# Sample states of a gated linear attention layer, contracted in two rounds of four per head

## Chip, core and metric

The kernel runs on one core of one Trainium2 chip. The metric is the device time of one execution in microseconds. The core's engines are named as the profile names them: PE multiplies matrices (PEld is its weight load, PEq its sequencer), DVE and ACT do elementwise work, POOL here mainly issues transfers, SP issues the other transfers.

## The reference

One inference step of a trunk with two layers, for a prompt of 256 tokens and for 8 samples of one token each, all with the same weights. Layer 0 mixes by pooling, layer 1 by gated linear attention; each is followed by an MLP with squared ReLU, and each of the four parts by a layer norm. What the change touches is the attention of the 8 samples. There are 4 heads with keys of 256 and values of 512, and each sample brings a state S of 256 x 512 for each head:

```
proj = x @ w_in;  q, k, v, og, gk_low = split(proj)
log_a = log_sigmoid(gk_low @ w_gate_up + gate_bias) / 16
# one token of a sample, per head
S_new = exp(log_a)[:, None] * S + outer(k, v)       # an output: new_gla_sample
o     = (q / 16) @ S_new
# then, for prompt and samples
o = rms_norm(o) * norm_w * silu(og);  y = o @ w_out
```

The prompt's attention is computed in chunks and gives its own state; the change leaves that as it is.

## The kernel before

**Layout.** Activations lie transposed, features on the 128 partitions and 264 columns (256 prompt tokens and 8 samples). The weights are a stream of 1 MB units, each 128 output features by 2048 inputs: 128 units for the first MLP, 64 for attention (48 of w_in, 16 of w_out), 128 for the second MLP. A unit is loaded by SP into `raw` (two buffers), and each half is split into a rounded part `whi` (ACT, L132) and a rest `wlo` (DVE, L133), six buffers each. The activations are split in the same way, and `mm3` (L145 to L147) makes three products for each of a unit's 16 blocks: 48 products a unit, one behind the other on PE.

**Order of the work.** PE runs in the order in which the program writes its instructions. For the other engines and for SP's and POOL's queues a scheduler fixes the order ahead of the run, from program order and its own estimates of when things are ready. Within `project`, after each 12 products, `slot()` advances every generator in the list `background` to its next `yield`. All the attention work that is not a product of weights is written as such generators: `normalise` and `gate_up`, then `chain` for the prompt (one head after the other), `samples` for the samples (one head after the other, each after its values are `turned`) and `rms`. A `yield` is therefore a wait of 12 products on PE, and what a generator issues on PE stands between two groups of 12. A head's k, q and v are eight units, 32 slots.

**The samples of a head.** `turn` transposes the values and their rests to `vs`, 16 rows by 512. For each of the eight samples: the state is loaded as one tile of 2 x 512 columns (the 256 keys are two halves of 128 partitions), ACT multiplies it by the decay (L596), PE spreads one sample's value over all partitions by a product with a column of `pick` (L615, into the one buffer of the PSUM bank "mc"), DVE adds k times that value to each half (L618), POOL stores the new state (L619), and three slots later `contract` (L610) multiplies it with q: two products of 32 weight columns (q in `qpad`, one of them not zero) and 512 moving columns, which go to a group of 32 PSUM partitions in the bank "mb", the group being the sample's number modulo four. Then the state of the sample after next is loaded. There are three such tiles. The products of this part are float32 and appear as two records each; those of `mm3` and L615 are float32r and appear as one.

**The gate's low rank product** (`gate_low`, L391) comes once, ahead of this: 32 float32 products of 32 weight columns, written so that four successive ones go to the four groups of PSUM partitions.

Of the kernel before, what the change touches and what calls it, by code (L numbers as in the profile page):

```python
# [6 lines left out]
F32 = mybir.dt.float32  # L7
F32R = mybir.dt.float32r
# [5 lines left out]
P = 128  # L14
D = 2048
KT = D // P
NP = 256
# [34 lines left out]
def _body(ctx, tc, nc, a, o, stop):  # L52
# [26 lines left out]
    def prm(name, i):  # L79
        return par[:, OFF[name] + i:OFF[name] + i + 1]  # L80

    # two sets of 16 tiles in two float32r parts; a pair of tiles is one slot of a set
    def hslot(s, i, shape, dt, name):
        return hp.tile(shape, dt, name=name, tag=f"{s}{i}")

    class Parts:
# [4 lines left out]
            for i in pairs:  # L91
                self.fresh(i)

        def fresh(self, i):
            th = hslot(self.s, i, [P, 2, NX], F32R, "hh")
            tl = hslot(self.s, 8 + i, [P, 2, NX], F32R, "hl")
            self.pairs[i] = th, tl
            for e in range(2):
                self.hi[2 * i + e], self.lo[2 * i + e] = th[:, e], tl[:, e]
# [1 line left out]
        def pair(self, m):  # L101
            return self.pairs[m // 2]

# [1 line left out]
    units = []  # L105

    def mlp_units(l):
# [75 lines left out]
        V.scalar_tensor_tensor(t, v, EPS, t, ALU.add, ALU.mult)  # L183
        V.scalar_tensor_tensor(out, t, 1.5, y0, ALU.add, ALU.mult)

    # ---- layer norm over the partitions of all tiles of Z + the last products.
    # d = z - c with c the mean of the first half; y = (d r - m) g + b. The next products take
    # g d, with g and b as two more columns, and are put right by r and m where they are read.
    class Norm:
        def __init__(self, name, x, ahead=1):  # L190
            self.g, self.b = name.replace("_", "_g"), name.replace("_", "_b")
# [165 lines left out]
    def gla(gctx, norm, xp, x, hg):  # L357
        gp = gctx.enter_context(tc.tile_pool(name="gp", bufs=1))
        masks = gp.tile([P, 576], U8, name="masks")
        wup = gp.tile([P, HEADS * DK], F32, name="wup", tag="s0", bufs=3)  # L360
        nwh = gp.tile([P, 4], F32, name="nwh")
        mf = gp.tile([P, 576], F32, name="mf", tag="s0", bufs=3)
        nc.gpsimd.dma_start(mf, a["masks"])
        V.tensor_copy(masks, mf)
        nc.sync.dma_start(wup, a["wup"])
        V.tensor_scalar(nwh, par[:, OFF["norm_w"]:OFF["norm_w"] + 4], 0.5, None, ALU.mult)
        rr = [gp.tile([P, N], F32, name=f"rr{i}") for i in range(2)]
        sa = gp.tile([P, 8, NS], F32, name="sa")
# [8 lines left out]
        wg = gp.tile([P, KT * 32], F32, name="wg", tag="st", bufs=2)  # L377
        low = gp.tile([P, N], F32, name="low", tag="st", bufs=2)
        nc.sync.dma_start(wg, a["wgk"])
        pick = gp.tile([2 * NS, NS], F32R, name="pick")  # L380
        G.tensor_tensor(pick, ident[:2 * NS, :NS], ident[:2 * NS, NS:2 * NS], op=ALU.add)

        # gate: log_a * 16 = min(gk, 0) - ln(1 + exp(-|gk|)); the low rank in four groups of columns,
        # summed by the product with the gate's weights
        def gate_low():
            ps = bank("mc")[:, :NX]
            for j in range(4):
# [8 lines left out]
        def gate_up():  # L396
            tc.keep_in_program_order(S.preload_act_table_set("natural_log_exp_and_others"))
            for t in range(8):
                yield
                while norm.done <= t:  # L400
                    yield
                ps = bank("ma")[:, :N]
                PE.matmul(ps, lhsT=wup[:, t * P:(t + 1) * P], rhs=low, start=True, stop=True)
                b = prm("gate_bias", t)
                e = wtile()
                S.activation(e, ps, AF.Abs, bias=b)
                S.activation(e, e, AF.Exp, scale=-1.0)
                S.activation(e, e, AF.Ln, bias=1.0)
                V.tensor_scalar(LA[:, t], ps, b, 0.0, ALU.add, ALU.min)
                V.tensor_tensor(LA[:, t], LA[:, t], e, op=ALU.subtract)  # L410
            S.activation(sa, LA[:, :, NP:], AF.Exp, scale=SCALE)
# [7 lines left out]
        class Head:  # L419
# [64 lines left out]
            def value(self, t, ps, raw):  # L484
                v = wtile()
                evacuate(v, ps, raw)

                vp = work.tile([P, 2 * NS], F32R, name="vp", bufs=4)
                V.tensor_copy(vp[:, :NS], v[:, NP:])
                V.tensor_tensor(vp[:, NS:], v[:, NP:], vp[:, :NS].bitcast(F32), op=ALU.subtract)  # L490

                def turn():
                    if t == 0:
                        self.vtok = [hslot(hg, 8 + 2 * self.h + b, [P, DV], F32, "vtok") for b in range(2)]
                        self.vs = gp.tile([2 * NS, DV], F32R, name="vs", bufs=2)
                    tp = bank("ma")
                    for b in range(2):
                        PE.transpose(tp[:, b * P:b * P + P], v[:, b * P:b * P + P], ident)  # L498
                    PE.transpose(tp[:2 * NS, NP:NP + P], vp.bitcast(F32), ident)
                    c = slice(t * P, t * P + P)  # L500
                    for b in range(2):
                        V.tensor_copy(self.vtok[b][:, c], tp[:, b * P:b * P + P])
                    S.copy(self.vs[:, c], tp[:2 * NS, NP:NP + P])
                    self.turned = t + 1

                if not raw:
                    later(2, turn)
                else:
                    self.turns = getattr(self, "turns", []) + [turn]
                    if t == 3:  # L510
                        for e, fn in enumerate(self.turns):
                            later(2 + e, fn)
# [53 lines left out]
            def rms(self):  # L566
# [18 lines left out]
                self.normed = True  # L585
                yield

            def samples(self):
                h = self.h
                s0s = {}  # L590

                def load(b):
                    s0s[b] = gp.tile([P, 2, DV], F32, name="s0", bufs=3)
                    nc.sync.dma_start(s0s[b], a["st"][h, b])
                    for hf in range(2):
                        S.mul(s0s[b][:, hf], s0s[b][:, hf], sa[:, 2 * h + hf, b:b + 1])  # L596

                load(0)
                load(1)
                while self.turned < 4:  # L600
                    yield
                for r in range(2):
                    V.tensor_copy(qpad[:, :, 4 * r:4 * r + 4, r], self.q[:, :, NP + 4 * r:NP + 4 * r + 4])
                yield
                op = bank("mb")

                def contract(b):
                    c, r = b % 4, b // 4
                    for hf in range(2):
                        PE.matmul(op[32 * c:32 * c + 32], lhsT=qpad[:, hf, b], rhs=s0s[b][:, hf],  # L610
                                  start=r == 0 and hf == 0, stop=r == 1 and hf == 1, tile_position=(0, 32 * c))

                for b in range(NS):
                    vb = bank("mc")
                    PE.matmul(vb, lhsT=pick[:, b:b + 1].broadcast_to([2 * NS, P]), rhs=self.vs, start=True, stop=True)  # L615
                    s0 = s0s[b]
                    for hf in range(2):
                        V.scalar_tensor_tensor(s0[:, hf], vb, self.k[:, hf, NP + b:NP + b + 1], s0[:, hf], ALU.mult, ALU.add)  # L618
                    nc.gpsimd.dma_start(o["ngs"][h, b], s0)  # L619
                    yield  # L620
                    yield
                    yield
                    contract(b)
                    if b + 2 < NS:
                        load(b + 2)
                    for _ in range(PACE_B[b % 2]):
                        yield
                os_ = gp.tile([P, DV], F32, name="os", tag="st", bufs=2)
                S.copy(os_, op)
                yield  # L630
                yield
                tp = bank("ma")
                for t in range(4):
                    PE.transpose(tp[:, t * P:t * P + P], os_[:, t * P:t * P + P], ident)
                tv = tp.rearrange("p (t c r) -> p t r c", t=4, c=4)
                V.tensor_copy(self.oT[:, :, NP:].rearrange("p t (r c) -> p t r c", r=2), tv[:, :, :2])
                self.sampled = True
# [64 lines left out]
        for h in range(HEADS):  # L702
            for t in range(4):
# [1 line left out]
                while not heads[h].normed:  # L705
                    slot()
                if t == 0:
                    gated.fresh(2 * h)
                    gated.fresh(2 * h + 1)
                heads[h].gate(t, ps, gated)  # L710
        assert not background and not pending
        return gated

# [1 line left out]
    xs = Parts("a")  # L715
    with tc.tile_pool(name="poolp", bufs=2) as pp:
        band, xt = {}, {}
# [75 lines left out]
    ln = mlp(0, ln, xs, Parts("b"), lambda: Parts("a"))  # L793
    if stop == "mlp0":
        return dump(ln)
# [1 line left out]
    with ExitStack() as gctx:  # L797
        xr = Parts("b")
        gated = gla(gctx, ln, ln.x, xr, "a")
    for m in range(KT):  # L800
        S.mul(Z[m], xr.hi[m][:, :N].bitcast(F32), ALPHA)
        V.scalar_tensor_tensor(Z[m], xr.lo[m][:, :N].bitcast(F32), ALPHA, Z[m], ALU.mult, ALU.add)
    xs = Parts("b")
    tc.keep_in_program_order(S.preload_act_table(AF.Abs_reciprocal_sqrt))
    ln = Norm("mix_1", xs)
    for m in range(KT):
        ln.add(project(gated))
    if stop == "gla":
        return dump(ln)
    ln = mlp(1, ln, xs, Parts("a"), None)  # L810
# [95 lines left out]
```

## Time and profile before

| | |
|---|---|
| time, median of 3 runs | 2137.87 us (2137.3 to 2138.28) |
| span of the profiled execution | 2137.0 us |
| PE busy | 2112.2 us, 99% of the span |
| DVE busy | 1255.9 us, 59% |
| ACT busy | 1081.8 us, 51% |
| HBM | 362.65 MB read, 22.14 MB written |

The span is that of one profiled execution, from its first to its last instruction; its time as the runs count it is not shown apart from that, and the median of the runs stands 0.87 us above the span. Busy times are unions of the records of an engine. A PE record is longer than the pace at which PE takes the next one, since matmuls are pipelined; the pace is read from start to start. One record of L145 lasts 288 ns in the mean, for example.

### The profile page before, as it was taken

What the parts mean: (1) busy time and instruction counts of PE and PEld (TensorE: products, weight loads), DVE (VectorE), ACT (ScalarE), POOL (GpSimd) and SP (SyncE); (2) the same over time, 40 slices, a digit from 0 to 9 for tenths busy, and PEclk for the clock granted to TensorE, in tenths of its full rate; (3) what the DMA queues carried; (4) which work ended last, traced back from release to release, by engine and by line L of the source; (5) the groups of instructions that cost most, each with busy time, mean ns of one, the idle gap of its engine ahead of it and who ended that gap; (6) DMA issues with size and microseconds to landing.
All of it is one profiled execution on the core that took longest, in us unless ns stands there. A gap on an engine that the chain in (4) does not pass through costs nothing.

```text
span 2137.0 us, 38691 instructions
## 1 busy us (share of the span) xinstructions
PE 2112.2 (99%) x16436; PEld 2029.0 (95%) x16436; DVE 1255.9 (59%) x1964; ACT 1081.8 (51%) x1650; POOL 37.1 (2%) x96
## 2 busy tenths in 40 slices
PE   8999999999999999999999999999999999999996
PEld 7999999999999999987878799999999999999996
DVE  3966444444544578856566667876444444444565
ACT  3657354345335456645545555557355345435543
POOL 0000000000000000000000010000000000000000
PEclk9999999999999999999999999999999999999998
DMA  6554555555554454555555544455555555555442
GB/s 233 179 182 180 180 181 181 180 179 178 177 178 178 178 178 158 188 208 211 202 198 199 206 163 175 169 178 177 180 181 180 181 180 180 179 178 178 178 178 81
DMA packets 62189, 386.18 MB, mean 181 GB/s; under 512 B 6752, under 2 KB 11104, under 8 KB 20528
## 3 DMA queue, kind: packets, MB, share of 16 engines
q1 hardware_dynamic: 56480, 363.27, 48.1%
q0 software_dynamic: 5392, 20.28, 2.4%
q8 instruction: 128, 2.10, 0.4%
q14 instruction: 45, 0.37, 0.1%
q10 hardware_dynamic: 144, 0.16, 0.0%
HBM read 362.65 MB, written 22.14 MB: 180 GB/s over the span
## 4 chain that ended last, share of the span: by engine, by line
PE 97%; DVE 1%; DMA 1%; ACT 1%; SPq 0%; issue 0%; ACTq 0%; DVEq 0%
PE ps L145 30%; PE ps L147 29%; PE ps L146 29%; PE mb L610 3%; PE ma L464 1%; PE ma L561 1%; PE mc L615 1%; DMA xt<-in_xt 0%; PE ps L756 0%; PE ma L517 0%; DMA raw<-in_w 0%; SPq L728 0%; DVE wlo L133 0%; ACT hh L245 0%; PE ma L498 0%
## 5 line engine op out<-in xcount | busy, mean ns | idle before, releaser
L145 PE MATMUL ps<-hh,whi 128*128 128x264 f32 (+1 forms) x5120 | 1476.6, 288 | 0.0
L147 PE MATMUL ps<-hh,wlo 128*128 128x264 f32 (+1 forms) x5120 | 1461.3, 285 | 0.0
L146 PE MATMUL ps<-hl,whi 128*128 128x264 f32 (+1 forms) x5120 | 1460.5, 285 | 0.0
L133 DVE TENSOR_TENSOR wlo<-raw,whi 128x1024 fp32r<-128x1024 f32 x640 | 783.5, 1224 | 617.1 <-ACT whi L132 614.1
L132 ACT CAST whi<-raw 128x1024 fp32r<-128x1024 f32 x640 | 670.9, 1049 | 898.6 <-PE ps L146 861.5
L145 PEld LDWEIGHTS ps<-hh,whi 128*128 128x128 f32 x5120 | 965.6, 189 | 36.9 <-issue 33.4
L146 PEld LDWEIGHTS ps<-hl,whi 128*128 128x128 f32 x5120 | 968.7, 189 | 2.0 <-issue 1.2
L147 PEld LDWEIGHTS ps<-hh,wlo 128*128 128x128 f32 x5120 | 967.5, 189 | 0.0
L178 DVE TENSOR_TENSOR hl<-wt,hh 128x264 fp32r<-128x264 f32 x192 | 81.6, 432 | 16.2 <-ACT hh L177 10.5
L177 ACT CAST hh<-wt 128x264 fp32r<-128x264 f32 x192 | 78.3, 410 | 9.2 <-DVE wt L643 5.1
L349 DVE TENSOR_TENSOR zt<-zt,ps 128x264 f32<-128x264 f32 x96 | 41.2, 429 | 64.9 <-PE ps L147 64.7
L618 DVE SCALAR_TENSOR_TENSOR s<-mc,k,s 128x512 f32<-128x512 f32 x64 | 46.1, 746 | 31.7 <-PE mc L615 31.2
L610 PE MATMUL mb<-s,qpad 128*32 128x512 f32 x128 | 60.9, 598 | 0.0
L338 ACT ACTIVATE wt<-wt 128x264 f32<-128x264 f32 x128 | 54.4, 425 | 4.0
L337 ACT ACTIVATE wt<-ps,par 128x264 f32<-128x264 f32 x96 | 45.6, 475 | 0.0
L596 ACT ACTIVATE s<-s,sa 128x512 f32<-128x512 f32 x64 | 43.3, 715 | 1.6 <-DMA s<-in_st 1.6
L210 DVE SCALAR_TENSOR_TENSOR zt<-ps,zt 128x264 f32<-128x264 f32 x48 | 20.6, 430 | 38.1 <-PE ps L147 38.1
L610 PEld LDWEIGHTS mb<-s,qpad 128*32 128x32 f32 x128 | 11.4, 109 | 24.5 <-issue 18.3
L252 ACT ACTIVATE wt<-zt 128x264 f32<-128x264 f32 x60 | 23.4, 412 | 17.6 <-DVE zt L210 17.6
L756 PE MATMUL ps<-px,pw 128*128 128x264 f32 x128 | 30.6, 399 | 0.0
L756 PEld LDWEIGHTS ps<-px,pw 128*128 128x128 f32 x128 | 25.1, 199 | 4.3
L301 ACT ACTIVATE wt<-zt,par 128x264 f32<-128x264 f32 x48 | 27.4, 601 | 1.1 <-DVE zt L300 1.1
(167 smaller groups left out, 852.6 us busy)
## 6 DMA issues: line engine op xcount, KB each, us to landing
raw<-in_w SPq DMA_DIRECT2D x256, 1024.0 KB, 4.7
raw<-in_win SPq DMA_DIRECT2D x48, 1024.0 KB, 4.9
s<-in_st SPq DMA_DIRECT2D x32, 512.0 KB, 3.4
out_ngs<-s POOLq DMA_DIRECT2D x32, 512.0 KB, 3.2
raw<-in_wout SPq DMA_DIRECT2D x16, 1024.0 KB, 4.8
pw<-in_pw SPq DMA_DIRECT2D x4, 1024.0 KB, 9.5
xt<-in_xt SPq DMA_DIRECT2D x3, 768.0 KB, 8.3
out_y<-zt SPq DMA_DIRECT2D x8, 264.0 KB, 2.2
```

The lines of the kernel that those rows point to most:

```text
L132: S.copy(hi, src)
L133: V.tensor_tensor(lo, src, hi.bitcast(F32), op=ALU.subtract)
L145: PE.matmul(ps, lhsT=whi, rhs=xh, start=start, stop=False)
L146: PE.matmul(ps, lhsT=whi, rhs=xl, start=False, stop=False)
L147: PE.matmul(ps, lhsT=wlo, rhs=xh, start=False, stop=stop_)
L177: S.copy(x.hi[m][:, :N], src)
L178: V.tensor_tensor(x.lo[m][:, :N], src, x.hi[m][:, :N].bitcast(F32), op=ALU.subtract)
L337: S.activation(t, project(x)[:, :N], AF.Relu, bias=bias)
L338: S.activation(t, t, AF.Square)
L610: PE.matmul(op[32 * c:32 * c + 32], lhsT=qpad[:, hf, b], rhs=s0s[b][:, hf], start=r == 0 and hf == 0, stop=r == 1 and hf == 1, tile_positi ...
L618: V.scalar_tensor_tensor(s0[:, hf], vb, self.k[:, hf, NP + b:NP + b + 1], s0[:, hf], ALU.mult, ALU.add)
L756: PE.matmul(ps[:, :N], lhsT=w[:, c], rhs=px[2 * g + k // 2][:, k % 2], start=k == 0, stop=k == 3)
```

## The change

The states of a head are taken in two rounds of four samples. Each state is two tiles of 512 columns from a set of nine, loaded and stored in halves. The decays are issued apart from the loads, just ahead of a sample's broadcast. The contractions of a round stand together: the first halves of the four samples, one slot later the second halves, four products side by side in the four groups of PSUM partitions. The next four loads follow. The broadcast's two operands get 128 rows: `pick` and `vs` are full tiles, zero below row 16. `vs` moves into slots of the set "a", and for that the first two gated tiles of head 0 move into the places of its k and q, so that the pool `gp` stays open until the products with w_out are written. The gate's weights and the masks, which share the states' buffers, are loaded in halves. The sums per head are the same. Hunks that only drop comments are left out.

```diff
-        def fresh(self, i):
-            th = hslot(self.s, i, [P, 2, NX], F32R, "hh")
+        def fresh(self, i, th=None):
+            if th is None:
+                th = hslot(self.s, i, [P, 2, NX], F32R, "hh")
             tl = hslot(self.s, 8 + i, [P, 2, NX], F32R, "hl")
...
         masks = gp.tile([P, 576], U8, name="masks")
-        wup = gp.tile([P, HEADS * DK], F32, name="wup", tag="s0", bufs=3)
+        half = lambda name: gp.tile([P, DV], F32, name=name, tag="s0", bufs=9)
+        wup = [half("wup") for _ in range(2)]
         nwh = gp.tile([P, 4], F32, name="nwh")
-        mf = gp.tile([P, 576], F32, name="mf", tag="s0", bufs=3)
-        nc.gpsimd.dma_start(mf, a["masks"])
-        V.tensor_copy(masks, mf)
-        nc.sync.dma_start(wup, a["wup"])
+        for c in (slice(0, 448), slice(448, 576)):
+            mf = half("mf")[:, :c.stop - c.start]
+            nc.gpsimd.dma_start(mf, a["masks"][:, c])
+            V.tensor_copy(masks[:, c], mf)
+        for e in range(2):
+            nc.sync.dma_start(wup[e], a["wup"][:, e * DV:(e + 1) * DV])
         V.tensor_scalar(nwh, par[:, OFF["norm_w"]:OFF["norm_w"] + 4], 0.5, None, ALU.mult)
...
         nc.sync.dma_start(wg, a["wgk"])
-        pick = gp.tile([2 * NS, NS], F32R, name="pick")
-        G.tensor_tensor(pick, ident[:2 * NS, :NS], ident[:2 * NS, NS:2 * NS], op=ALU.add)
+        pick = gp.tile([P, NS], F32R, name="pick")
+        G.memset(pick.bitcast(F32), 0.0)
+        G.tensor_tensor(pick[:2 * NS], ident[:2 * NS, :NS], ident[:2 * NS, NS:2 * NS], op=ALU.add)
         def gate_low():
...
                 ps = bank("ma")[:, :N]
-                PE.matmul(ps, lhsT=wup[:, t * P:(t + 1) * P], rhs=low, start=True, stop=True)
+                PE.matmul(ps, lhsT=wup[t // 4][:, t % 4 * P:(t % 4 + 1) * P], rhs=low, start=True, stop=True)
                 b = prm("gate_bias", t)
...
                         self.vtok = [hslot(hg, 8 + 2 * self.h + b, [P, DV], F32, "vtok") for b in range(2)]
-                        self.vs = gp.tile([2 * NS, DV], F32R, name="vs", bufs=2)
+                        self.vs = hslot(hg, self.h % 2, [P, DV], F32R, "vs")
+                        V.memset(self.vs.bitcast(F32), 0.0)
                     tp = bank("ma")
...
                         V.tensor_copy(self.vtok[b][:, c], tp[:, b * P:b * P + P])
-                    S.copy(self.vs[:, c], tp[:2 * NS, NP:NP + P])
+                    S.copy(self.vs[:2 * NS, c], tp[:2 * NS, NP:NP + P])
                     self.turned = t + 1
...
                 def load(b):
-                    s0s[b] = gp.tile([P, 2, DV], F32, name="s0", bufs=3)
-                    nc.sync.dma_start(s0s[b], a["st"][h, b])
+                    s0s[b] = [half("s0") for _ in range(2)]
                     for hf in range(2):
-                        S.mul(s0s[b][:, hf], s0s[b][:, hf], sa[:, 2 * h + hf, b:b + 1])
-                load(0)
-                load(1)
+                        nc.sync.dma_start(s0s[b][hf], a["st"][h, b][:, hf])
+                def decay(b):
+                    for hf in range(2):
+                        S.mul(s0s[b][hf], s0s[b][hf], sa[:, 2 * h + hf, b:b + 1])
+                for b in range(4):
+                    load(b)
                 while self.turned < 4:
...
                     V.tensor_copy(qpad[:, :, 4 * r:4 * r + 4, r], self.q[:, :, NP + 4 * r:NP + 4 * r + 4])
+                decay(0)
                 yield
                 op = bank("mb")
-                def contract(b):
-                    c, r = b % 4, b // 4
+                for r in range(2):
+                    if r:
+                        decay(4)
+                        yield
+                    for b in range(4 * r, 4 * r + 4):
+                        vb = bank("mc")
+                        PE.matmul(vb, lhsT=pick[:, b:b + 1].broadcast_to([P, P]), rhs=self.vs, start=True, stop=True)
+                        for hf in range(2):
+                            s0 = s0s[b][hf]
+                            V.scalar_tensor_tensor(s0, vb, self.k[:, hf, NP + b:NP + b + 1], s0, ALU.mult, ALU.add)
+                            nc.gpsimd.dma_start(o["ngs"][h, b][:, hf], s0)
+                        yield
+                        if b % 4 < 3:
+                            decay(b + 1)
+                            yield
+                            yield
+                    yield
                     for hf in range(2):
-                        PE.matmul(op[32 * c:32 * c + 32], lhsT=qpad[:, hf, b], rhs=s0s[b][:, hf],
-                                  start=r == 0 and hf == 0, stop=r == 1 and hf == 1, tile_position=(0, 32 * c))
-                for b in range(NS):
-                    vb = bank("mc")
-                    PE.matmul(vb, lhsT=pick[:, b:b + 1].broadcast_to([2 * NS, P]), rhs=self.vs, start=True, stop=True)
-                    s0 = s0s[b]
-                    for hf in range(2):
-                        V.scalar_tensor_tensor(s0[:, hf], vb, self.k[:, hf, NP + b:NP + b + 1], s0[:, hf], ALU.mult, ALU.add)
-                    nc.gpsimd.dma_start(o["ngs"][h, b], s0)
-                    yield
-                    yield
-                    yield
-                    contract(b)
-                    if b + 2 < NS:
-                        load(b + 2)
-                    for _ in range(PACE_B[b % 2]):
+                        for c in range(4):
+                            b = 4 * r + c
+                            PE.matmul(op[32 * c:32 * c + 32], lhsT=qpad[:, hf, b], rhs=s0s[b][hf],
+                                      start=r == 0 and hf == 0, stop=r == 1 and hf == 1, tile_position=(0, 32 * c))
+                        yield
+                    if r == 0:
+                        for b in range(4, NS):
+                            load(b)
+                        yield
                         yield
...
                 if t == 0:
-                    gated.fresh(2 * h)
-                    gated.fresh(2 * h + 1)
+                    for e in range(2):
+                        gated.fresh(2 * h + e, gp.tile([P, 2, NX], F32R, name="kq"[e] + "0") if h == 0 else None)
                 heads[h].gate(t, ps, gated)
...
         gated = gla(gctx, ln, ln.x, xr, "a")
-    for m in range(KT):
-        S.mul(Z[m], xr.hi[m][:, :N].bitcast(F32), ALPHA)
-        V.scalar_tensor_tensor(Z[m], xr.lo[m][:, :N].bitcast(F32), ALPHA, Z[m], ALU.mult, ALU.add)
-    xs = Parts("b")
-    tc.keep_in_program_order(S.preload_act_table(AF.Abs_reciprocal_sqrt))
-    ln = Norm("mix_1", xs)
-    for m in range(KT):
-        ln.add(project(gated))
+        for m in range(KT):
+            S.mul(Z[m], xr.hi[m][:, :N].bitcast(F32), ALPHA)
+            V.scalar_tensor_tensor(Z[m], xr.lo[m][:, :N].bitcast(F32), ALPHA, Z[m], ALU.mult, ALU.add)
+        xs = Parts("b")
+        tc.keep_in_program_order(S.preload_act_table(AF.Abs_reciprocal_sqrt))
+        ln = Norm("mix_1", xs)
+        for m in range(KT):
+            ln.add(project(gated))
     if stop == "gla":
```

## Rows read from the trace of the kernel before

**Rows 1.** The page's first line, and the chain that ended last by engine and line
```profile
span 2137.0 us, 38691 instructions
...
PE 97%; DVE 1%; DMA 1%; ACT 1%; SPq 0%; issue 0%; ACTq 0%; DVEq 0%
PE ps L145 30%; PE ps L147 29%; PE ps L146 29%; PE mb L610 3%; PE ma L464 1%; PE ma L561 1%; PE mc L615 1%; DMA xt<-in_xt 0%; PE ps L756 0%; PE ma L517 0%; DMA raw<-in_w 0%; SPq L728 0%; DVE wlo L133 0%; ACT hh L245 0%; PE ma L498 0%
```

**Rows 2.** Windows: length, busy us (records) of each engine, clock, DMA share, GB/s
```profile
100.00:775.00 675.00, 675.00 (x5495) 675.00 (x5494) 352.99 (x424) 331.61 (x455) 4.79 (x16) 1.00 0.51 180
870.00:1242.00 372.00, 371.72 (x2433) 299.12 (x2431) 244.27 (x512) 193.71 (x343) 21.43 (x40) 1.00 0.55 199
```

**Rows 3.** Waits of the engines, 870 to 1242: us in total, times, longest
```profile
ACT whi L132 <- PE ps L146: 91.9, 46, 5.3
```

**Rows 4.** Timelines of SP and PE: start, us, where the first attention unit begins
```profile
801.29 0.33 SPq L126 DMA_DIRECT2D raw<-in_win  x1
...
822.43 0.29 PE L145 MATMUL ps<-hh,whi 128*128 128x266 f32 x1
```

**Rows 5.** Timeline of PE around a broadcast: start, us, instruction
```profile
905.82 0.28 PE L147 MATMUL ps<-hh,wlo 128*128 128x264 f32 x1
906.03 0.49 PE L615 MATMUL mc<-vs,pick 16*128 16x512 f32 x1
906.45 0.39 PE L145 MATMUL ps<-hh,whi 128*128 128x264 f32 x1
906.68 0.28 PE L146 MATMUL ps<-hl,whi 128*128 128x264 f32 x1
```

**Rows 6.** The samples' groups: busy us, mean ns of one, idle before
```profile
L618 DVE SCALAR_TENSOR_TENSOR s<-mc,k,s 128x512 f32<-128x512 f32 x64 | 46.1, 746 | 31.7 <-PE mc L615 31.2
L610 PE MATMUL mb<-s,qpad 128*32 128x512 f32 x128 | 60.9, 598 | 0.0
L596 ACT ACTIVATE s<-s,sa 128x512 f32<-128x512 f32 x64 | 43.3, 715 | 1.6 <-DMA s<-in_st 1.6
...
L619 POOL DMA_DIRECT2D out_ngs<-s x32 | 17.1, 533 | 430.0 <-DVE s L618 419.0 <-DVE vtok L502 11.0
...
L615 PE MATMUL mc<-vs,pick 16*128 16x512 f32 x32 | 15.7, 490 | 0.0
```

**Rows 7.** Timeline of PE around a contraction
```profile
911.77 0.28 PE L147 MATMUL ps<-hh,wlo 128*128 128x264 f32 x1
911.98 1.90 PE L610 MATMUL mb<-s,qpad 128*32 128x512 f32 x4
913.82 0.39 PE L145 MATMUL ps<-hh,whi 128*128 128x264 f32 x1
914.04 0.28 PE L146 MATMUL ps<-hl,whi 128*128 128x264 f32 x1
```

**Rows 8.** Timeline of PE around the low rank product, first and last of eight groups
```profile
835.96 0.29 PE L147 MATMUL ps<-hh,wlo 128*128 128x266 f32 x1
836.17 0.66 PE L391 MATMUL mc<-hh,wg 128*32 128x266 f32 x8
...
839.33 0.63 PE L391 MATMUL mc<-hl,wg 128*32 128x266 f32 x8
839.90 0.39 PE L145 MATMUL ps<-hh,whi 128*128 128x266 f32 x1
840.12 0.28 PE L146 MATMUL ps<-hl,whi 128*128 128x266 f32 x1
```

**Rows 9.** Waits of SP's queue, 870 to 1242: us in total, times, longest
```profile
SPq L126 <- DVE wlo L133: 89.8, 14, 10.4
...
SPq L594 <- PE mb L610: 45.1, 25, 3.5
```

**Rows 10.** DMA issues: count, KB each, median us from issue to landing
```profile
raw<-in_win SPq DMA_DIRECT2D x48, 1024.0 KB, 4.9
s<-in_st SPq DMA_DIRECT2D x32, 512.0 KB, 3.4
```

## The prediction

> **What bounds the kernel now.** I read the chain that ended last first. Nearly all of it is PE: 97% of the span is matmul time, and the product lines L145 to L147 alone make 88% [rows 1]. The change touches two of its smaller entries: the contraction of the samples' states (L610, 3%) and the value broadcast (L615, 1%). Then the windows [rows 2]: in the attention stage, 870 to 1242 us, PE is busy for 371.72 of 372 us, while DVE is busy for 244 and ACT for 194; the DMA share is 0.55. The clock stands at 1.00, the upper of its two levels, here and in the MLP stretch above it. So every microsecond taken from PE in this stage comes off the end, as long as nothing else becomes late. That second condition is read from the waits: in the stage ACT's casts of weights wait 91.9 us for PE to give back a buffer [rows 3], so weights are ahead of PE and not behind. How far ahead: the load of the first attention unit is issued at 801.29 and its first product starts at 822.43, 21.1 us later [rows 4].
>
> The unit of PE time is the pace of the plain products: 675 us over 5495 records, 0.123 us each [rows 2]. A slot (12 products) is 1.47 us without anything in between.
>
> **The broadcasts.** Each of the 32 is one record, but its cost is read from start to start. Between the product at 905.82 and the one at 906.68 lie one product of 0.123, the broadcast, and another product of 0.123: 0.86 - 0.25 = 0.61 us [rows 5]. The product behind it takes 0.23 from its start to the next one instead of 0.123, and the start before it is also late (0.21). The broadcast differs from its neighbours by its 16 rows [rows 6]; at 128 rows, by the full `pick` and the zeroed `vs`, I expect it to be one more record in the stream. Its cost by columns is then 512/264 x 0.123 = 0.24 us. Bounds: 0.61 (the rows are not the reason) and 0.24. I take 0.24, since the excess sits at both edges, where the shape changes. Gain: 32 x 0.37 = 11.8 us.
>
> The Trainium skill says the same in "TensorEngine Tiling (Array Packing)", Tiling Modes, and more sharply: a change of tiling mode drains the engine. By that rule, too, the edges go and the broadcast costs what its columns cost. It also speaks for the toll that every contraction below still pays.
>
> **The contractions.** Before, one sample's contraction is four records in one column group (two halves of two records). From 911.77 to 914.04 lie 2.27 us, less two products 2.02 [rows 7]. 32 of them: 64.8 us. The records themselves follow each other at (913.82 - 911.98)/4 = 0.46 us, so nothing overlaps, and the edges cost some 0.2.
>
> After, the same 128 records come in 16 bursts of eight (one half of four samples, a column group each). The trace has this arrangement once, in the gate's low rank product L391: four groups, 32 weights columns, 266 columns moving, two records per product, eight bursts of eight without a break [rows 8]. The first burst starts at 836.17, the eighth at 839.33: 0.451 us for eight records. By columns, 512/266 x 0.451 = 0.87 us for a burst. The edges: from 835.96 to 840.12 are 4.16 us, less two products 3.91, less 8 x 0.451, leaves 0.30. A burst of the new kernel has both edges, since a slot of products lies between the two halves: 1.17 us. 16 of them are 18.7 us. Bounds: nothing overlaps, 8 x 0.46 + 0.30 = 3.98 each, 63.7 in all (no gain); and the edges vanish too, 13.9. I take 18.7, because L391 is the same shape but for the columns. Gain: 64.8 - 18.7 = 46.1 us.
>
> **What is added or moved, off PE.** Two halves per state instead of one tile: 64 loads and 64 stores of 256 KB instead of 32 each of 512 KB. POOL issues 32 more at 0.53 us [rows 6], 17 us on an engine that has 21 us of work in the stage [rows 2]. SP issues 32 more. The bytes are the same. Four memsets of `vs` on DVE are no dearer than the 0.75 us of a 128x512 pass [rows 6], 3 us at most. DVE's 244 us become 247 in a stage of 372 - 58 = 314, a share of 0.79; ACT's 194 us a share of 0.62. Neither fills. The halves of `wup` and the masks add a DMA and a copy each before the stage; `pick` gets one memset on POOL; the gated tiles in the place of k0 and q0 and the longer life of the pool issue nothing. All of this is put at nothing, covered by PE's stream; uncovered it would be the 3 us of DVE.
>
> **The loads, which do move.** Before, a state's load was issued when the contraction of the sample before last was over (SP waited for L610 25 times, 45.1 us [rows 9]), with a sample in reserve. Now a round frees four samples' halves at once and the next round's loads go out together, after its contractions. Count the slots of the new order: with the second burst in slot n, the loads are emitted in n+1, the decays of the first sample in n+3, its broadcast in n+4, the second broadcast in n+7. The broadcasts share one PSUM bank, so PE stops at n+7 if DVE has not read the first one by then. DVE needs the load (3.4 us to landing for 512 KB [rows 10]), two decays (2 x 0.72 on ACT) and two passes (2 x 0.75) [rows 6]: 6.3 us from the release. Seven slots are at least 7 x 1.47 = 10.3 us. With the chain's products between them they are longer: before, the three slots from the broadcast at 906.03 to the contraction at 911.98 take 5.95 us, less the broadcast 1.78 each [rows 5, 7], so seven take 12.5. The margin is 4.0 to 6.2 us, and I put the waits at 1 us in all. The first of these eight rounds has no such wait (head 0 loads before its values come), so seven are exposed. On the other side, 2 MB of states ahead of a load of weights in SP's order costs at most 4 x 3.4 = 13.6 us, and a load of weights has 21.1 - 4.9 = 16.2 us [rows 4, 10] for that and for its split.
>
> At the end of a round the first burst comes two slots behind the last broadcast, where it was three. Two slots are 2.9 us and more; the first half's pass is done about 0.5 + 0.75 us after the broadcast. Put at nothing; if DVE is a whole weight split behind, a fraction of a microsecond eight times.
>
> **The sum.** 11.8 + 46.1 = 57.9 us. The profiled span is 2137.0 us [rows 1]; the median of the runs is 2137.87, so 0.9 us lie around the span or between executions. 2137.0 - 57.9 + 0.9 + 1.0 = 2081.0 us.
>
> **Rivals.**
> - Late loads, in part. In the stage SP stood 14 times, 6.4 us in the mean, with a load of weights that waited for a split [rows 9]. A state's load queued behind such a one waits those 6.4 and the 4.9 of its transfer, 11.3 us, which is 5.1 to 7.3 more than the margin. In two to four of the seven rounds: 10 to 29 us, 2091 to 2110. For it: SP's order is fixed ahead and its waits are real. Against it: before, most state loads left at once when the contraction ended.
> - Slower than before by the same mechanism. It has to give back 57.9 us in seven rounds, 8.3 each, so each round's loads must come 8.3 + 6.2 = 14.5 us late (12.3 if slots are bare). SP's longest wait for a split in the stage is 10.4, with a transfer 15.3 [rows 9, 10]. It would need about that in every round: 2138 and more.
> - The column groups overlap less at 512 columns than at 266. Two at a time gives 4 x 0.46 + 0.30 = 2.1 us a burst, 34 us in all, 15.5 more than forecast: 2097.
> - The Trainium skill, "TensorE: Matmul & The Clock Gate", Part 3, gives 2.38 times for three column tiles and 3.07 for four row tiles at 512 columns, short of the four times that L391 shows. With 3.07 a burst would be an estimated 8 x 0.46/3.07 + 0.30 = 1.5 us, which by itself puts the time at some 2086. Its place is between the forecast and the rival above.
> - The contractions do not overlap at all, the change doing only the broadcasts: 2137.9 - 11.8 - 1.1 = 2125.
> - The broadcast's 0.61 us is not a matter of rows: 2081 + 11.8 = 2093.
>
> **Chances.** Forecast, 2076 to 2087: 0.62. Late loads in part, 2087 to 2110: 0.17. Less overlap, 2086 to 2097: 0.08. Broadcasts unchanged, 2093: 0.05. No overlap, 2125: 0.03. Slower: 0.03. The rest, faster than 2075: 0.02. From 2075 to 2098 lie the forecast, the two cases around 2093 and over half of the late loads, about 0.85. A measurement of this kernel can tell 0.2%, 4 us. Faster 0.95, same 0.02, slower 0.03.
>
> **What would show it.** Right: the bursts of eight in the PE timeline start at most 0.9 us before the next record, the line's busy time falls to under 20 us, the start after a broadcast is 0.24 us later and the product behind it again 0.12; the stage is 57 to 58 us shorter and PE still busy all through it. Wrong: PE idle before a broadcast, released by the pass on DVE, with ACT's decay before it released by the load (late loads); a burst of 1.8 us or more (overlap); a broadcast followed by a product of 0.23 (rows). The prediction as a whole fails if PE is not the bound in the shorter stage, which would be seen as products waiting for weights.

## The result and the profile after

The changed kernel takes 2082.80 us (2082.34 to 2083.68, four runs) against 2138.07 us before, a ratio of 0.9741 with a 95% interval of 0.9730 to 0.9753. The forecast was 2081.0 with a range of 2075 to 2098, so the time lies 1.8 us above the forecast.

The page's first line and its chain by engine, of the changed kernel; line numbers have moved (products L146 to L148, broadcast L624, contraction L638):

```profile
span 2080.8 us, 38806 instructions
...
PE 94%; DVE 3%; ACT 1%; DMA 1%; SPq 0%; issue 0%; ACTq 0%; DVEq 0%
PE ps L146 30%; PE ps L148 30%; PE ps L147 30%; PE ma L469 1%; DVE wlo L134 1%; PE mb L638 1%; PE ma L567 1%; DMA xt<-in_xt 0%; PE ps L774 0%; ACT whi L133 0%; PE mc L624 0%; DMA raw<-in_w 0%; PE ma L523 0%; SPq L746 0%; DMA s<-in_st 0%
```

The span is 56.2 us shorter. The contraction has gone from 3% to 1% of the chain, the broadcast from 1% to 0% [rows 1]. In which stretch the time was saved is read between two marks on PE: the first product of the first attention unit, and the norm's product over `lnm` after half of w_out.

```profile
822.44 0.29 PE L146 MATMUL ps<-hh,whi 128*128 128x266 f32 x1
...
1256.89 0.61 PE L224 MATMUL ma<-lnm,ones 128*128 128x264 f32 x2
```

The first mark stands where it stood [rows 4]; the second stood at 1313.17 before. From mark to mark are 434.45 us instead of 490.74: all of the gain, 56.3 us, lies in this stretch. It is called the stage below, and it is the better measure between runs, since the first plain product of the kernel starts anywhere from 62.1 to 64.9 us in the traces of this study, ahead of any changed code. Each run has one trace, so a stage is the length in one execution.

One broadcast of the changed kernel in the timeline of PE:

```profile
891.62 0.28 PE L148 MATMUL ps<-hh,wlo 128*128 128x264 f32 x1
891.74 0.39 PE L624 MATMUL mc<-vs,pick 128*128 128x512 f32 x1
891.97 0.29 PE L146 MATMUL ps<-hh,whi 128*128 128x264 f32 x1
892.10 0.29 PE L147 MATMUL ps<-hl,whi 128*128 128x264 f32 x1
```

From 891.62 to 892.10 are 0.48 us, less two products 0.23: the broadcast costs what its columns cost (0.24 at the pace of the plain products), and both edges of [rows 5] are gone. The first round's two bursts, in the same view:

```profile
906.77 0.28 PE L148 MATMUL ps<-hh,wlo 128*128 128x264 f32 x1
906.98 1.06 PE L638 MATMUL mb<-s,qpad 128*32 128x512 f32 x8
907.97 0.39 PE L146 MATMUL ps<-hh,whi 128*128 128x264 f32 x1
908.20 0.28 PE L147 MATMUL ps<-hl,whi 128*128 128x264 f32 x1
...
909.64 1.07 PE L638 MATMUL mb<-s,qpad 128*32 128x512 f32 x8
```

From 906.77 to 908.20 are 1.43 us, less two products 1.19 for eight records, where four took 2.02 [rows 7]. The line's busy time says the same; the contraction's was 60.9 us before [rows 6]:

```profile
L638 PE MATMUL mb<-s,qpad 128*32 128x512 f32 x128 | 17.1, 605 | 0.0
...
L624 PE MATMUL mc<-vs,pick 128*128 128x512 f32 x32 | 14.8, 464 | 0.0
```

The windows of the shorter stage (length, busy time and records by engine, clock, DMA share, GB/s) show PE still busy nearly throughout, DVE and ACT with nearly the same work in less time, and the DMA share at 0.67 instead of 0.55 [rows 2]:

```profile
870.00:1185.00 315.00, 314.17 (x2426) 287.31 (x2425) 244.44 (x524) 196.43 (x344) 38.48 (x71) 1.00 0.67 233
```

### The profile page after: what moved, and what is told of

It is laid out like the page before. It is cut to its first block, busy times and chain, and to the rows that moved or that the text cites. A ratio compares the mean times of both kernels' runs of the same rounds, so it can differ in the third digit from the quotient of the medians.

```text
span 2080.8 us, 38806 instructions
## 1 busy us (share of the span) xinstructions
PE 2055.9 (99%) x16436; PEld 2018.4 (97%) x16436; DVE 1254.3 (60%) x1969; ACT 1082.0 (52%) x1650; POOL 54.9 (3%) x130
## 4 chain that ended last, share of the span: by engine, by line
PE 94%; DVE 3%; ACT 1%; DMA 1%; SPq 0%; issue 0%; ACTq 0%; DVEq 0%
PE ps L146 30%; PE ps L148 30%; PE ps L147 30%; PE ma L469 1%; DVE wlo L134 1%; PE mb L638 1%; PE ma L567 1%; DMA xt<-in_xt 0%; PE ps L774 0%; ACT whi L133 0%; PE mc L624 0%; DMA raw<-in_w 0%; PE ma L523 0%; SPq L746 0%; DMA s<-in_st 0%
## 5 line engine op out<-in xcount | busy, mean ns | idle before, releaser
L146 PE MATMUL ps<-hh,whi 128*128 128x264 f32 (+1 forms) x5056 | 1454.0, 288 | 0.0
L148 PE MATMUL ps<-hh,wlo 128*128 128x264 f32 (+1 forms) x5056 | 1443.1, 285 | 0.0
L146 PEld LDWEIGHTS ps<-hh,whi 128*128 128x128 f32 x5056 | 953.7, 189 | 16.5 <-issue 15.8
L148 PEld LDWEIGHTS ps<-hh,wlo 128*128 128x128 f32 x5056 | 955.4, 189 | 0.0
L627 DVE SCALAR_TENSOR_TENSOR s<-mc,k,s 128x512 f32<-128x512 f32 x64 | 45.8, 744 | 3.4 <-PE mc L624 3.4
L628 POOL DMA_DIRECT2D out_ngs<-s x64 | 34.7, 542 | 351.0 <-DVE s L627 343.3
L246 ACT ACTIVATE hh<-zt,par 128x264 fp32r<-128x264 f32 x48 | 24.1, 511 | 5.6 <-DVE zt L237 3.6
```

What stands on the lines that cost most here:

```text
L146: PE.matmul(ps, lhsT=whi, rhs=xh, start=start, stop=False)
L148: PE.matmul(ps, lhsT=wlo, rhs=xh, start=False, stop=stop_)
L627: V.scalar_tensor_tensor(s0, vb, self.k[:, hf, NP + b:NP + b + 1], s0, ALU.mult, ALU.add)
```

## The experiments

Medians are set beside 2082.80 us for the changed kernel and some 2138.6 for the one before. All ratios are to the kernel before.

### Broadcasts of 16 rows in the changed kernel

```diff
-PE.matmul(vb, lhsT=pick[:, b:b + 1].broadcast_to([P, P]), rhs=self.vs, ...)
+PE.matmul(vb, lhsT=pick[:16, b:b + 1].broadcast_to([16, P]), rhs=self.vs[:16], ...)
```

> The changed kernel with the broadcasts alone put back to 16 rows. My theory: a broadcast of 16 rows pays at both edges for a change of the array's shape, 0.61 us instead of the 0.23 us that the changed kernel's trace shows, so 32 x 0.38 = 12.2 us come back: 2095 us (2094 to 2096). Rival, the cost lies in the contractions around it and not in the rows: 2083 us, within 2 us of the changed kernel.

Measured: 2094.57 us, ratio 0.9795 (0.9781 to 0.9808). The stage is 446.22 us (823.02 to 1269.24), 11.8 more than in the changed kernel. The rows are the reason. 11.8 is a little under 32 x 0.38 = 12.2. Seven of the 32 broadcasts stand behind a small product of the prompt's chain; these cost 0.27 us in the mean in the changed kernel and 0.61 here, by the same reading from start to start, so they give 0.34 each.

### 128 rows alone, in the kernel before

```diff
-self.vs = gp.tile([2 * NS, DV], F32R, name="vs", bufs=2)
+self.vs = gp.tile([P, DV], F32R, name="vs", bufs=2)
+V.memset(self.vs.bitcast(F32), 0.0)
...
-PE.matmul(vb, lhsT=pick[:, b:b + 1].broadcast_to([2 * NS, P]), rhs=self.vs, ...)
+PE.matmul(vb, lhsT=pick[:, b:b + 1].broadcast_to([P, P]), rhs=self.vs, ...)
```

(`pick` is a zeroed tile of 128 rows here too.)

> The kernel before with 128 rows in the broadcasts as its only change. My theory: 12.2 us less than before, 2126 us (2125 to 2127), the two parts of the change adding up. Rival, the gain of the rows needs the new order (in the old one PE waits for something else, or the edge is paid to the contraction anyhow): 2132 to 2138 us.

Measured: 2126.21 us, ratio 0.9944 (0.9931 to 0.9958); the stage is 478.78 us (821.39 to 1300.17), 12.0 less than before. The rows give 12.0 us alone and 11.8 on top of the rest, so the two parts of the change add up.

### 64 rows

The edit is that of 16 rows with 64 in its place.

> The changed kernel with 64 rows in the broadcasts. My theory: any number of rows that makes the array another shape than its neighbours' pays the same at the edges, 0.61 us as with 16 rows: 2094.6 us (2093.5 to 2096). Rival, the cost falls with the rows that are used, half of it gone at 64: 2088 us (2086 to 2090).

Measured: 2095.18 us, ratio 0.9795 (0.9781 to 0.9808), the stage 446.03 us (821.89 to 1267.92). One broadcast of this kernel in PE's timeline:

```profile
891.48 0.28 PE L148 MATMUL ps<-hh,wlo 128*128 128x264 f32 x1
891.69 0.50 PE L624 MATMUL mc<-vs,pick 64*128 64x512 f32 x1
892.11 0.39 PE L146 MATMUL ps<-hh,whi 128*128 128x264 f32 x1
892.34 0.29 PE L147 MATMUL ps<-hl,whi 128*128 128x264 f32 x1
```

0.86 - 0.25 = 0.61 us, as with 16. 64 rows cost as much as 16. As far as these three heights show (16, 64, 128), the toll hangs on being unlike the neighbours, at both edges (0.21 and 0.23 from start to start instead of 0.12), and not on how unlike.

### Rounds as they are, but one sample to a slot

```diff
-for hf in range(2):
-    for c in range(4):
-        b = 4 * r + c
+for c in range(4):
+    b = 4 * r + c
+    for hf in range(2):
         PE.matmul(op[32 * c:32 * c + 32], lhsT=qpad[:, hf, b], rhs=s0s[b][hf], ...)
     yield
```

> The changed kernel, rounds, halves, loads and 128 rows as they are, but the four samples of a round are contracted one to a slot (both halves of one sample, then 12 products of weights, then the next sample), so that no two groups of columns stand together. My theory: the whole gain of the contraction comes from groups that stand side by side; a lone sample costs the 2.03 us of the kernel before, so 32 x 2.03 - 16 x 1.19 = 45.9 us come back: 2128.7 us (2127 to 2131). Rival, part of the gain comes from the new order of loads, stores and decays: 2085 to 2120 us.

Measured: 2128.39 us, ratio 0.9951 (0.9938 to 0.9963). The stage is 479.82 us (822.38 to 1302.19), 45.4 more than in the changed kernel, and the line is back at its old cost:

```profile
L638 PE MATMUL mb<-s,qpad 128*32 128x512 f32 x128 | 60.9, 598 | 0.0
```

The kernel before with 128 rows alone has a stage of 478.78 us. This one, with the new loads, halves and rounds added to that, has 479.82: by themselves they bring nothing, and the gain of the contraction is the standing side by side.

### Two samples side by side

```diff
-for hf in range(2):
-    for c in range(4):
-        ...
+for c0 in (0, 2):
+    for hf in range(2):
+        for c in (c0, c0 + 1):
+            ...
     yield
```

> The changed kernel with two samples side by side instead of four: in the first slot of a round's end both halves of the samples 0 and 1 (two groups of columns, eight records), in the second those of 2 and 3. Theory A, a burst costs what its longest group costs, four records of 0.43 us, and 0.32 for the edges, however many groups stand beside it: 2.05 us each, 16 of them 32.8 instead of 19.0 us, so 13.8 more: 2096.6 us (2095.5 to 2098). Theory B, eight records cost 1.19 us as in the changed kernel whatever their groups: 2083 us.

Measured: 2095.95 us, ratio 0.9799 (0.9786 to 0.9813); the stage is 447.55 us (821.65 to 1269.20), 13.1 more than in the changed kernel. Theory A holds. The first burst of the first round in this kernel:

```profile
905.99 0.28 PE L148 MATMUL ps<-hh,wlo 128*128 128x264 f32 x1
906.20 1.91 PE L639 MATMUL mb<-s,qpad 128*32 128x512 f32 x8
908.04 0.39 PE L146 MATMUL ps<-hh,whi 128*128 128x264 f32 x1
908.26 0.28 PE L147 MATMUL ps<-hl,whi 128*128 128x264 f32 x1
```

2.27 us, less two products 2.02: eight records in two groups cost what four in one group did [rows 7], and eight in four groups 1.19. What counts is how many records the group with the most of them has, 0.43 us each (the records of one group start that far apart in this trace), and 0.3 for the edges.

### Both halves in one burst, in two orders

```diff
+yield
 for hf in range(2):
     for c in range(4):
         b = 4 * r + c
         PE.matmul(op[32 * c:32 * c + 32], lhsT=qpad[:, hf, b], rhs=s0s[b][hf], ...)
-    yield
+yield
```

> The changed kernel with both halves of a round in one burst of sixteen records, in the slot where the second half stood; the order inside is the same (first the four first halves, then the four second halves). My theory: the 0.32 us of edges is paid per burst, so eight bursts fewer give 2.6 us: 2080.2 us (2079.5 to 2081), a burst of 16 taking 1.74 + 0.32 = 2.06 us. Rival, the 1.19 us of a burst is all the work of eight records and no toll of the edges: 2.38 us a burst, 2083 us.

Measured: 2080.93 us, ratio 0.9732 (0.9719 to 0.9746). The stage is 432.68 us (821.95 to 1254.62), 1.8 less than in the changed kernel. The medians differ by 1.9 us, which is under the 4 us that the measurement can tell; the trace shows the burst itself. Sixteen records run from 907.96 to the next product's start at 909.81.

```profile
907.74 0.28 PE L148 MATMUL ps<-hh,wlo 128*128 128x264 f32 x1
907.96 1.92 PE L639 MATMUL mb<-s,qpad 128*32 128x512 f32 x16
909.81 0.39 PE L146 MATMUL ps<-hh,whi 128*128 128x264 f32 x1
910.04 0.28 PE L147 MATMUL ps<-hl,whi 128*128 128x264 f32 x1
```

2.30 less two products are 2.05 us, as expected; the edges are paid per burst. Of the 2.6 us, 0.8 went back into waits for ACT and DVE elsewhere in the stage: PE waits for 1.5 us there, against 0.7 in the changed kernel.

With the loops over `c` and `hf` exchanged in that burst, so that one sample's two halves stand behind one another and each group of columns comes once:

> As the run with one burst, but ordered by sample: the first and second half of one sample behind one another in one group of columns, then the next sample. My theory, PE starts records in order and a record waits for the one before it in its own group, so only one record overlaps at each change of group: 13 steps of 0.43 us + 0.32 = 5.9 us a round, 3.9 more than in one burst by halves, 31 us in eight rounds: 2111 us (2105 to 2115). Rival, PE looks ahead and fills the four groups in whatever order they come: 2080 us, as with the other order.

Measured: 2081.81 us, ratio 0.9735 (0.9721 to 0.9748). My theory is wrong and the rival right. The stage is 433.56 us (820.50 to 1254.06), 0.9 more than with the other order, of which PE's waits for ACT and DVE make 0.5. The burst:

```profile
906.30 0.28 PE L148 MATMUL ps<-hh,wlo 128*128 128x264 f32 x1
906.52 1.94 PE L639 MATMUL mb<-s,qpad 128*32 128x512 f32 x16
908.39 0.39 PE L146 MATMUL ps<-hh,whi 128*128 128x264 f32 x1
908.62 0.28 PE L147 MATMUL ps<-hl,whi 128*128 128x264 f32 x1
```

2.32 less two products are 2.07 us, 0.02 more than in the other order and far from 5.9. A group's four records, which follow one another in the program, do not hold up the groups behind them. The starts show it: four records start within 0.04 us (906.516 to 906.556) and the next four 0.45 later, as in the other order, while a lone sample's four records start 0.43 to 0.45 apart. The first four are 0.013 us apart here and 0.007 in the other order, so the two orders did reach PE as two different streams.

### No slots between the two rounds

```diff
 if r:
     decay(4)
-    yield
...
     load(b)
-yield
-yield
```

> The changed kernel with the three slots between the two rounds of a head taken out: the loads of the second round, the decay of its first sample and its first broadcast are issued in one slot, and the second broadcast comes four slots behind the last burst instead of seven. By the margins of my prediction, with the landing that the changed kernel's trace shows (5.5 us, then 1.4 of decays and 1.5 of passes, against 4 x 1.78 = 7.1 us), PE waits 1.3 us for the second broadcast in each of four rounds, 2088 us, more if the casts of weights on ACT stand behind a late decay. Rival, by the trace's times of the first state alone (its halves are free a slot earlier, after the first burst; its decays end 4.0 us behind the end of the second burst, 1.5 more for the passes): no wait, 2083 us (2082 to 2084).

Measured: 2085.28 us, ratio 0.9750 (0.9737 to 0.9763); the stage is 436.67 us (823.31 to 1259.98), 2.2 more than in the changed kernel. The broadcasts in question do not wait: in the first head the passes on DVE end at 916.5 and the second broadcast starts at 919.44. So the rival is right about them, but not about the time. PE's waits in this stage, in all:

```profile
PE mc L623 <- ACT vs L509: 0.6, 1, 0.6
PE ma L523 <- ACT zt L525: 0.4, 1, 0.4
PE mb L637 <- DVE s L626: 0.4, 1, 0.4
PE ma L504 <- ACT vs L509: 0.2, 1, 0.2
```

They are 1.6 us, where the changed kernel has 0.7 (0.5 for `vs` ahead of L652, 0.2 ahead of L504). The wait for DVE costs more than its 0.4 us, because it cuts a burst in two:

```profile
1142.35 1.06 PE L637 MATMUL mb<-s,qpad 128*32 128x512 f32 x6
1143.78 1.04 PE L637 MATMUL mb<-s,qpad 128*32 128x512 f32 x2 [0.37 <-DVE s L626]
1144.75 0.39 PE L146 MATMUL ps<-hh,whi 128*128 128x264 f32 x1
```

Six records start in time and the last sample's two 1.4 us later, so this burst costs 2.60 us from start to start instead of 1.19. That is most of the 2.2 us. The last state is not late: its decays end at 1129.7, before its broadcast at 1138.97, and its pass stands behind other work on DVE, a split that waits 1.06 us for ACT among it. So this loss is in the order of the work on DVE and ACT, and no late load is seen in it. For the 0.6 us ahead of a broadcast that stays open: ACT waits 9.3 us for states between 870 and 1190 us here, against 2.6 in the changed kernel. Neither theory had these paths.

### States as whole tiles

```diff
-half = lambda name: gp.tile([P, DV], F32, name=name, tag="s0", bufs=9)
+state_ = lambda name: gp.tile([P, 2, DV], F32, name=name, tag="s0", bufs=4)
...
-    s0s[b] = [half("s0") for _ in range(2)]
-    for hf in range(2):
-        nc.sync.dma_start(s0s[b][hf], a["st"][h, b][:, hf])
+    s0s[b] = state_("s0")
+    nc.sync.dma_start(s0s[b], a["st"][h, b])
```

(`wup` and the masks are one load each again, and a state is one store.)

> The changed kernel with a state as one tile of 2 x 512 columns again, four of them, loaded and stored by one transfer each as before the change; rounds, bursts and rows as changed. A state's place is then free only after the second burst, a slot later than a first half's, and there is no ninth half. Theory A, halves make nothing: the changed kernel's first decays end some 3.7 us ahead of the first broadcast, which covers a slot of 1.8: 2083 us (2082 to 2084.5). Theory B, the halves are what keeps the loads in time: waits as in the run without the slots between the rounds, 2085 us or more.

Measured: 2083.16 us with a wide spread (2077.70 to 2085.08), ratio 0.9733 (0.9720 to 0.9746): by the time, nothing to tell from the changed kernel. The profiled execution is the slowest of the five. Its stage is 437.99 us (821.37 to 1259.36), 3.5 more than the changed kernel's, and it shows what a late load does. Timelines of ACT and PE in this kernel (brackets give the idle time before and what ended it), and the window in which the products follow at half their pace:

```profile
1018.07 1.33 ACT L604 ACTIVATE s<-s,sa 128x512 f32<-128x512 f32 x2 [2.32 <-DMA s<-in_st]
1019.30 0.24 ACT L507 CAST vs<-ma 16x128 fp32r<-16x128 f32 x1
```
```profile
1019.60 1.12 PE L649 MATMUL ma<-ident,os 128*128 128x128 f32 x4 [2.41 <-ACT vs L507]
...
1020.73 0.42 PE L147 MATMUL ps<-hl,whi 128*128 128x264 f32 x1
1020.95 0.42 PE L148 MATMUL ps<-hh,wlo 128*128 128x264 f32 x1
```
```profile
1020.30:1022.40 2.10, 2.10 (x11) 2.10 (x11) 1.65 (x3) 1.82 (x5) 0.00 (x0) 0.50 0.25 105
```

ACT stands 2.32 us with a decay whose state has not landed. The copy of a head's values out of PSUM is queued behind it, and PE waits 2.41 us for the bank that this copy frees. The wait costs more than itself: behind it the granted clock is 0.50, the lower of the two levels (1.2 GHz), and the products start 0.22 us apart instead of 0.123. The four transposes and the twelve products behind them take 3.37 us, where the changed kernel takes 1.96 for the same sixteen at clock 1.00. The 1.4 us of this and the 2.4 of the wait, less the 0.5 that the changed kernel waits in such a place, are 3.3 of the 3.5 us. The late load fits places that come free late: the next loads of states start 3.7 us behind the round's first burst here (1007.18 to 1010.91), and 1.1 in the changed kernel (1008.24 to 1009.31). The broadcasts of the states themselves were in time. Theory A is not refuted by the medians; the path is shown once, in one execution.

### A further slot ahead of the output's transposes

```diff
 S.copy(os_, op)
 yield
 yield
+yield
```

(with one burst for both halves)

> The run with one burst for both halves, and one slot more ahead of the transposes of the samples' output. In the run with one burst PE still waits some 0.9 us ahead of one of these transposes, for ACT's copy of the values that stands in the same PSUM buffers. My theory: that wait goes: 2080 us (2079 to 2081). Rival, it is off the path or comes back at the next user of these buffers: 2081 us, not to be told from the run with one burst.

Measured: 2081.99 us (2079.70 to 2083.44), ratio 0.9734 (0.9721 to 0.9747), no gain. The stage is 435.01 us (822.74 to 1257.75), 2.3 more than with one burst alone. PE's waits in it:

```profile
PE ma L505 <- DVE vp L495: 2.1, 2, 1.6
PE ma L523 <- ACT vs L509: 0.9, 1, 0.9
PE ma L504 <- ACT vs L509: 0.2, 1, 0.2
PE ma L523 <- ACT zt L525: 0.2, 1, 0.2
```

The rival's second half came true: the wait ahead of the transposes went, and others took its place, ahead of the transposes of the samples' values (L505) and of the prompt's products (L523). No version of this study beats the changed kernel by more than the measurement tells; one burst for both halves is 1.8 us shorter in the stage of its one trace.

## Why the prediction was right

**The bound.** It rested on PE being busy without a break in the stage and on nothing else becoming late. After the change PE is busy for 314.17 of 315 us there, and plain products never wait for weights. Of the 1.8 us between forecast and time, about half is the term for what lies around the span. It was put at 0.9 us, from the median of the runs and the span of one execution; where a run's time and its own span are set side by side it is some 1.8 (2082.59 us for a span of 2080.8). Two of the signs named were missed narrowly: a burst starts 0.99 us before the next record (at most 0.9 was named), and the stage is 56.3 us shorter (57 to 58).

**The broadcasts.** Forecast 0.61 to 0.24 us, a gain of 11.8 us. Measured 0.61 to 0.23, 11.8 by taking the rows back and 12.0 by changing them alone. The reason given, the edges and not the row count, is shown by 64 rows, which cost as much as 16. The Trainium skill, "TensorEngine Tiling (Array Packing)", Tiling Modes, says that a change of tiling mode drains TensorE. The three runs agree, with 0.61 us at 16 and at 64 rows against 0.23 at 128; the drain itself is seen in no trace.

**The contractions.** Forecast 1.17 us a burst, measured 1.19; forecast gain 46.1 us, measured 45.8 from the starts of all bursts (64.8 less 19.0) and 45.4 when the samples are contracted apart. The pace of 0.46 us a record in the prediction had part of the edges in it; records of one group start 0.43 apart. Scaling the low rank product's 0.451 us by columns gave 0.87 for eight records, and the shape alone was enough to carry it over. The Trainium skill, "TensorE: Matmul & The Clock Gate", Part 3, gives a factor of 3.07 for four row tiles and has none for four column tiles. Taken over to this burst it gave the estimate of 1.5 us, and that is not borne out: four samples apart take 8.1 us, side by side 2.4 in two bursts or 2.05 in one, the latter a factor of 4.0 with the edges counted.

**The loads.** The term was 1 us. The sum of the two gains by their events, 32 x (0.61 - 0.23) + 32 x 2.02 - 16 x 1.19 = 57.8 us, against 56.3 in the stage, leaves 1.5 us. That this is near the 1 us is in part luck. PE's waits in the stage rose only from 0.3 to 0.7 us, all of it for ACT's copies of the values and none for a state; where the other 1.1 us went, no run here shows. Two steps of the working did not hold either. The landing of a state was put at 3.4 us from the loads before; the median of the changed kernel's 64 loads is 5.5:

```profile
s<-in_st SPq DMA_DIRECT2D x64, 256.0 KB, 5.5
```

The 2.1 us more lie within the margin of 4.0 to 6.2. Besides, the first halves' places are free after the first burst, a slot ahead of what I counted: four of a round's loads start from 908.05 on, before the second burst at 909.64.

```profile
908.05 1.75 SPq L603 DMA_DIRECT2D s<-in_st  x4
```

And the place where PE would wait was put at the second broadcast of a round. In no run did a broadcast wait for a state. Where the loads were pressed, PE waited for ACT's copies out of PSUM and for DVE's passes, and a late load stood behind one such wait, in the run with whole states: 2.4 us of waiting and 1.4 at the lower clock. Of the 2.2 us of the run without the slots between the rounds, 1.4 lie in one burst that no late load held up. The rival of late loads is thus a path shown once, at some 3.5 us in one execution, not at 10 to 29.

## What to carry to other kernels

Look for small products that stand alone in a stream of full ones, and read them from start to start, with the product behind them: here a record of 0.49 us cost 0.61, and 0.23 once its operands were padded with zeros to the shape of the rest. Products of 32 columns belong side by side in different column groups, as many groups as there are, in one stretch; the price here was that of the group with the most records and one toll for the stretch. When transfers are grouped as well, follow every engine's queue from the instruction that waits for them: in the run with whole states the harm came not to the late state's own broadcast but to a copy that stood behind its decay.

## What the runs showed of the hardware

The order inside a burst does not matter: sixteen records of four groups took 2.05 us when the groups alternated and 2.07 when each group's four records stood together in the program, although in strict order only one record could have overlapped at each change of group (5.9 us). How far ahead such overlap reaches is not settled; across the 12 full products of a slot it does not, as the run with one sample to a slot shows. A broadcast of 64 rows cost the 0.61 us of one of 16. Once, PE stood still for 2.41 us in a stream at clock 1.00; the granted clock behind it was 0.50, and sixteen records took 3.37 us instead of 1.96.
